# Taps of a convolution spread over three attention heads, its low parts on another engine, and the first queries moved ahead

## The chip, the cores and the metric

The kernel runs on one core of one Trainium2 chip. The metric is the device time of one execution in microseconds (us), as the median of several runs. The engines are TensorE (PE; its weight loads are PEld), VectorE (DVE), ScalarE (ACT), GpSimd (POOL) and SyncE (SP).

## The reference

Two transformer blocks of width 1024 follow each other on 512 latent tokens, with 256 context tokens beside them. The first block has two layers, and the change lies in these. A layer normalises and modulates both token sets, projects them, and mixes them in three ways whose outputs are joined: differential attention with 4 heads, a pooling mixer, and a convolution over 31 taps with a gate before it and a layer norm behind it. The joined mix goes through an output projection, and a feed-forward part follows.

```python
u = a * sigmoid(b)                                  # 256 channels
y = depthwise_conv(u, dw_w, taps=31) + dw_b
conv = silu(layer_norm(y, ln_g, ln_b))
attn = (softmax(q0 k0') - lam * softmax(q1 k1')) v  # 4 heads, queries in blocks of 128
mix  = concat([rms_norm(attn), pool_mixer(u_pool), conv])
x    = x + g1 * (mix @ w_out)
x    = x + g2 * swiglu(modulate(rms_norm(x)))
```

The first layer also carries the context through mix and feed-forward; the second uses it for keys and values alone. The second block (another attention and a recurrence) is not touched.

## The kernel before

Every matrix product keeps 32-bit accuracy by three products: each operand is split into a rounded high part and a low part (the source less the high part), and `mm3` (L250) multiplies high by high, high by low and low by high. `split` (L326) makes the high part on ScalarE and the low part on VectorE, unless another engine is given. Weights are loaded by SyncE in halves, cast by ScalarE (L229) and their low parts taken by GpSimd (L231); `Weights.next` (L234) loads one weight ahead, and there are two buffers for a weight's high and low parts.

Tokens come in three groups of 256: "0" is the context, "1" and "2" the latents. `layer` (L993) of layer 0 begins with `start` (L433), which normalises, and computes the convolution's gate `g` for all tokens and its value `u` for the latents. The context part of `u` is left to the windows. `windows(l)` (L716) gives five lists of items: one before attention, and one for each head. Items are projections of queries and keys (`q0` to `q3`, one a head and token group), of values (`v0`, `v1`), of the pool input (`p`), slices of the modulation (`m`), convolution taps (`t`), the pool mixer (`pool`), the convolution's norm (`ln`), splits of the mix (`sp`) and output parts (`o`). Layer 1 computes the convolution's input at the end of the first list.

`attn` (L873) walks the 4 heads, with 6 query tiles of 128 each in layer 0 and 4 in layer 1. Before every tile it yields, and `layer` emits the next share of the head's list. A tile is `attn_scores` (scores on TensorE into the `s2t` banks, maxima `nmx` on VectorE L800, exponentials `e` on ScalarE L804, the combination of the two softmaxes on VectorE L845) and, one tile later, `attn_values` (transposes, the product with the values, the norm of the output `on` L863 with a square root on GpSimd L298). Queries and keys are normalised by `qk_norm` (L757 on: sums on VectorE L763, square root on GpSimd L298, products on VectorE and GpSimd) and turned on TensorE by `qk_turn` (L792).

The program's text is not the order of the instructions. A planner at build time simulates the engines with durations of its own and takes for each engine, of the instructions that are ready, the one with the best priority; that order is then fixed for every engine. The priority is the place in the text; `high_priority(n)` moves it n places ahead, and a negative n back. Attention is raised by 300.

A tap multiplies the shifted input `uc` by one weight and adds it to `mix[6]` or `mix[7]` (two halves of the channels, `ct` 0 and 1): one VectorE instruction (L665, the first of a half L663) over 783 columns in layer 0 and 512 in layer 1, 62 of them a layer. An item holds 4 taps, and taps are lowered by 1500. The lists of heads 0 and 1 hold 28 and 34 taps. The pool mixer (L612) sums shifted inputs on GpSimd with the `uc` tiles as scratch, and so behind all taps. `splits` (L1026) splits the finished mix for the output projection; output parts with the pool's and the convolution's half of the mix are emitted in head 3.

Of the kernel before, what the change touches and what calls it, by code (L numbers as in the profile page):

```python
# [14 lines left out]
ALU = mybir.AluOpType  # L15
# [11 lines left out]
WINDOWS = (2, 4, 8, 16)  # L27
TAPS = 31
PAD = TAPS // 2
CTX = slice(0, NCX)  # L30
LAT = slice(NCX, NT)

# [210 lines left out]
class K:  # L243
# [365 lines left out]

        return c if self.CW == NX + NCX + PAD and c < NCX else (c + PAD if self.CW != NX else c - NCX)  # L610

    def pool_mix(self, pa, l, ct):  # L612

        nc = self.nc
        add = lambda o, a, b: nc.gpsimd.tensor_tensor(out=o, in0=a, in1=b, op=ALU.add)
        segs, o = [], 0
        for L in ([NCX] if l == 0 else []) + [NX]:
            segs.append((L, self.up[ct][:, o:o + L + 16], self.up[ct][:, o + 8:o + 8 + L]))
            o += L + 16

        def means():
            for L, u, v in segs:
                s = [None] * 4
                prev, ln = u, L + 16
                for i in range(2 if ct == 0 else 4):
                    t = self.uc[i % 2]
                    r = slice(64, 128) if i == 2 * ct + 1 else slice(0, 128)
                    st = 1 << i
                    ln -= st
                    add(t[r, 0:ln], prev[r, 0:ln], prev[r, st:st + ln])  # L630
                    s[i], prev = t, t
                for hf in range(2):
                    i = ct * 2 + hf
                    sh = 8 - WINDOWS[i] // 2
                    r = slice(hf * 64, hf * 64 + 64)
                    tt = self.p_small.tile([128, 2, 8], F32, tag="edge", name="edge", bufs=2)
                    for e in range(2):
                        x0 = e * (L - 8)
                        ed = self.pv("edge", ct * 16 + e * 8, 8)[r]
                        nc.vector.tensor_tensor(out=tt[r, e], in0=s[i][r, sh + x0:sh + x0 + 8], in1=ed, op=ALU.mult)  # L640
                        nc.vector.tensor_tensor(out=tt[r, e], in0=tt[r, e], in1=v[r, x0:x0 + 8], op=ALU.subtract)
                    nc.vector.scalar_tensor_tensor(
                        out=v[r], in0=s[i][r, sh:sh + L], scalar=self.pv("invw", ct)[r], in1=v[r], op0=ALU.mult, op1=ALU.subtract)
                    for e in range(2):
                        nc.vector.tensor_copy(out=v[r, e * (L - 8):e * (L - 8) + 8], in_=tt[r, e])

        def weights():
            for L, _, v in segs:
                ps = self.ps([128, L])
                nc.tensor.matmul(ps, lhsT=self.PW[:, 128 * ct:128 * ct + 128], rhs=v, start=True, stop=True)  # L650
                nc.scalar.activation(out=v, in_=ps, func=AF.Identity, scale=self.pv(f"pscale{l}", ct))

        return [(0, means), (14, weights)]

    def conv_taps(self, pa, l, mix, ct, j0, j1):

        nc = self.nc
        W = self.CW
        m, u = mix[6 + ct][:, 0:W], self.uc[ct]
        dw = lambda j: self.DWH[:, ct * TAPS + j:ct * TAPS + j + 1]  # L660
        for j in range(j0, j1):
            if j == 0:
                nc.vector.tensor_scalar(out=m, in0=u[:, 0:W], scalar1=dw(0), scalar2=self.pv(f"dwb{l}", ct), op0=ALU.mult, op1=ALU.add)  # L663
            else:
                nc.vector.scalar_tensor_tensor(out=m, in0=u[:, j:j + W], scalar=dw(j), in1=m, op0=ALU.mult, op1=ALU.add)  # L665

    def conv_ln(self, pa, l, mix, c, L):

# [47 lines left out]
    def windows(self, l):  # L716

        gr = ("0", "1", "2") if l == 0 else ("1", "2")  # L720
        fm = lambda n: [(n, ct, g) for ct in "01" for g in gr]
        tm = lambda n: [(n, g) for g in "012"]
        taps = [("t", ct, j) for ct in "01" for j in range(0, TAPS, 4)]
        mod = lambda n: [("m",)] * n

        def merge(*ls):

            out = list(ls[0])
            for extra in ls[1:]:
                n, k, r = len(out), 0, []  # L730
                for i, it in enumerate(out):
                    r.append(it)
                    while k < len(extra) * (i + 1) // n:
                        r.append(extra[k])
                        k += 1
                out = r
            return out

        q0, v0 = tm("q0"), tm("v0")
        nm = self.MODS_MIX[l]  # L740
        conv = [it for g in ("01", "2") for n in "gu" for it in fm(n) if it[2] in g]
        return [
            [("u", ct, "0") for ct in "01"] + q0 + v0 if l == 0 else q0[:2] + v0[:2] + q0[2:] + v0[2:] + conv,
            merge(tm("q1") + fm("p"), taps[:7], mod(nm[0])),
            merge(tm("q2") + tm("v1"), taps[7:], mod(nm[1])),
            merge(tm("q3") + [("pool", 0), ("pool", 1)] + [("ln", g) for g in ((0, 1) if l == 0 else (1,))], mod(nm[2])),
            [("sp", int(g), 0) for g in gr] + [("x",)] + mod(nm[3])
            + merge([("o", int(g), m) for g in gr for m in range(KD)], [("sp", int(g), 1) for g in gr]),
        ]
# [76 lines left out]
    def attn_scores(self, pa, l, hd, g, i, qk, og):  # L826

        nc = self.nc
        nk = NCX if g == 0 else NT
        t = slice((2 * g + i) * 128, (2 * g + i) * 128 + 128)  # L830
        s = [self.s2([128, 1024]) for _ in range(2)]
        for n, (a, b) in enumerate(((0, 0), (0, 1), (1, 0))):
            for k0, k1 in ((0, min(nk, 512)), (512, nk)):
                for c in range(2):
                    r = slice(64 * c, 64 * c + 64)
                    if k1 > k0:
                        nc.tensor.matmul(s[c][:, k0:k1], lhsT=qk[r, 0, a, t], rhs=qk[r, 1, b, k0:k1], start=n == 0, stop=n == 2)  # L837
        ss = self.p_small.tile([128, 2], F32, tag="sa", name="sa", bufs=4)
        e = [self.softmax_exp(pa, s[c], nk, ss[:, c:c + 1], f"e{c}") for c in range(2)]

        w = self.p_small.tile([128, 2], F32, tag="rr", name="rr", bufs=4)
        nc.vector.reciprocal(out=w, in_=ss)
        nc.vector.tensor_copy(out=og["r0"][:, i:i + 1], in_=w[:, 0:1])
        nc.vector.scalar_tensor_tensor(out=w[:, 1:2], in0=ss[:, 0:1], scalar=self.LAM[l], in1=w[:, 1:2], op0=ALU.mult, op1=ALU.mult)
        nc.vector.scalar_tensor_tensor(out=e[0][:, 0:nk], in0=e[1][:, 0:nk], scalar=w[:, 1:2], in1=e[0][:, 0:nk], op0=ALU.mult, op1=ALU.add)  # L845
        return e[0], nk

    def attn_values(self, pa, l, hd, g, i, e, nk, v, og, mix):
# [23 lines left out]

    def attn(self, pa, l, qk, v, mix, done):  # L873

        prev = turn = None
        for hd in range(4):
            for g in range(0 if l == 0 else 1, 3):
                for i in range(2):
                    yield hd
                    if i == 0:  # L880
                        og = {n: self.p_small.tile([128, 2], F32, tag="g" + n, name=n, bufs=3) for n in ("r0", "ss")}
                    with self.tc.high_priority(300):
                        e, nk = self.attn_scores(pa, l, hd, g, i, qk[hd], og)
                        if turn is not None:
                            turn()
                        turn = self.attn_values(*prev) if prev is not None else None
                    prev = (pa, l, hd, g, i, e, nk, v[hd], og, mix)
                    if hd == 3 and i == 1 and g > (0 if l == 0 else 1):
                        done(g - 1)
        self.attn_values(*prev)()  # L890
        done(2)
# [101 lines left out]
    def layer(self, l, then):  # L993
# [8 lines left out]
        with self.pool(f"a{l}") as pa, self.pool(f"b{l}") as pb:  # L1002
# [4 lines left out]
            with self.pool(f"mix{l}") as pmix:  # L1007
# [18 lines left out]
                def splits(g, ks):  # L1026
                    for k in ks:
                        src = mix[k] if k not in (4, 5) else self.up[k - 4]
                        o = 8 if k in (4, 5) else 0
                        if g == 0:  # L1030
                            self.split(hmc[k][0], hmc[k][1], src[:, o:o + NCX])
                        else:
                            if full:
                                o += NCX + (16 if k in (4, 5) else 0 if k < 4 else PAD)
                            cs = slice(256 * g - 256, 256 * g)
                            self.split(hm[k][0][:, cs], hm[k][1][:, cs], src[:, o + cs.start:o + cs.stop])

                def issue(it):
                    name = it[0]
# [14 lines left out]
                        return self.mod_slot(*self.mods.pop(0))  # L1054
                    if name == "t":
                        def taps():
                            with self.tc.high_priority(-1500):
                                self.conv_taps(pa, l, mix, int(it[1]), it[2], min(it[2] + 4, TAPS))
                        return taps
                    if name == "pool":  # L1060
                        return self.pool_mix(pa, l, it[1])
                    if name == "ln":
                        return self.conv_ln(pa, l, mix, (0, NCX)[it[1]], (NCX, NX)[it[1]])
                    if name == "x":
# [695 lines left out]
```

## Time and profile before

| | |
|---|---|
| median of 3 runs | 2638.83 us |
| lowest and highest | 2630.06 and 2649.29 us |
| the profiled execution's own time | 2639.62 us |
| its span | 2637.8 us |
| PE busy | 2501.8 us, 95% of the span |
| DVE, ACT, POOL busy | 975.5, 910.5 and 1129.6 us |

Busy times are sums over an engine's instructions; a busy PE is not PE at its peak, so its granted clock (PEclk, as a share of full speed) is read beside it. Rows below are of this one execution, and their times count from the start of its span.

### The profile page before, as it was taken

What the parts mean: (1) busy time and instruction counts of PE and PEld (TensorE: products, weight loads), DVE (VectorE), ACT (ScalarE), POOL (GpSimd) and SP (SyncE); (2) the same over time, 40 slices, a digit from 0 to 9 for tenths busy, and PEclk for the clock granted to TensorE, in tenths of its full rate; (3) what the DMA queues carried; (4) which work ended last, traced back from release to release, by engine and by line L of the source; (5) the groups of instructions that cost most, each with busy time, mean ns of one, the idle gap of its engine ahead of it and who ended that gap; (6) DMA issues with size and microseconds to landing.
All of it is one profiled execution on the core that took longest, in us unless ns stands there. A gap on an engine that the chain in (4) does not pass through costs nothing.

```text
span 2637.8 us, 38665 instructions
## 1 busy us (share of the span) xinstructions
PE 2501.8 (95%) x15840; PEld 2131.7 (81%) x15840; DVE 975.5 (37%) x1941; ACT 910.5 (35%) x1909; POOL 1129.6 (43%) x956
## 2 busy tenths in 40 slices
PE   7889989999999999999989999999998899999998
PEld 5778779988888888877788777778887788888887
DVE  4897564121120224488542112123322756210113
ACT  4334444312112124333535223234444543422222
POOL 4544314433233334555326545445323344555553
PEclk8889989999999999999999999999999899999999
DMA  7113311323223232222224445343101021222221
GB/s 244 58 49 113 122 62 49 113 90 105 93 96 112 85 108 89 75 64 81 97 80 145 152 128 164 116 162 107 52 33 51 17 96 49 80 96 96 93 90 57
DMA packets 68977, 248.55 MB, mean 94 GB/s; under 512 B 7488, under 2 KB 10816, under 8 KB 67136
## 3 DMA queue, kind: packets, MB, share of 16 engines
q1 hardware_dynamic: 65568, 232.29, 27.1%
q10 hardware_dynamic: 3232, 13.79, 1.4%
q8 instruction: 125, 2.05, 0.3%
q14 instruction: 52, 0.43, 0.1%
HBM read 239.75 MB, written 6.29 MB: 93 GB/s over the span
## 4 chain that ended last, share of the span: by engine, by line
PE 48%; DVE 6%; ACT 2%; POOL 1%; DMA 1%; issue 1%; POOLq 0%; ACTq 0%; DVEq 0%; SPq 0%
PE s2t L258 6%; PE s2t L255 6%; PE s2t L259 6%; PE pj L255 5%; PE pj L258 5%; PE pj L259 5%; PE ap L820 2%; DVE mix L665 1%; PE ap L258 1%; PE ap L255 1%; PE ap L259 1%; PE s2t L1532 1%; PE s2t L837 1%; PE ap L344 1%; PE ap L816 1%; PE s L255 1%
## 5 line engine op out<-in xcount | busy, mean ns | idle before, releaser
L231 POOL TENSOR_TENSOR wlo<-raw,whi 128x512 fp32r<-128x512 f32 x564 | 731.2, 1329 | 698.8 <-ACT whi L229 698.5
L229 ACT CAST whi<-raw 128x512 fp32r<-128x512 f32 x576 | 319.7, 616 | 681.9 <-PE pj L258 237.4
L258 PE MATMUL s2t<-hl,whi 128*128 128x512 f32 (+1 forms) x1184 | 448.4, 379 | 0.9 <-POOL hl L429 0.9
L255 PE MATMUL s2t<-hh,whi 128*128 128x512 f32 (+1 forms) x1184 | 447.5, 379 | 0.9 <-ACT whi L229 0.9
L259 PE MATMUL s2t<-hh,wlo 128*128 128x512 f32 (+1 forms) x1184 | 447.0, 378 | 0.0
L255 PE MATMUL pj<-hh,whi 128*128 128x256 f32 (+1 forms) x1088 | 336.6, 311 | 9.9 <-ACT hh L426 3.3
L258 PE MATMUL pj<-hl,whi 128*128 128x256 f32 (+1 forms) x1088 | 331.4, 305 | 2.6 <-DVE hl L431 1.5
L259 PE MATMUL pj<-hh,wlo 128*128 128x256 f32 (+1 forms) x1088 | 330.5, 305 | 0.3 <-POOL wlo L231 0.3
L955 DVE TENSOR_TENSOR sg<-sg,s2t 128x512 f32<-128x512 f32 x66 | 45.4, 688 | 629.2 <-ACT sg L954 629.2
L255 PEld LDWEIGHTS s2t<-hh,whi 128*128 128x128 f32 x1184 | 223.0, 189 | 48.1 <-issue 1.6
L259 PEld LDWEIGHTS s2t<-hh,wlo 128*128 128x128 f32 x1184 | 223.0, 188 | 45.5 <-issue 1.2
L258 PEld LDWEIGHTS s2t<-hl,whi 128*128 128x128 f32 x1184 | 223.0, 188 | 44.8 <-POOL hl L429 1.1
L255 PEld LDWEIGHTS pj<-hh,whi 128*128 128x128 f32 x1088 | 209.3, 193 | 27.5 <-ACT hh L426 4.7
L328 POOL TENSOR_TENSOR gl<-sg,gh 128x512 fp32r<-128x512 f32 (+1 forms) x66 | 97.7, 1480 | 303.9 <-ACT gh L327 303.9
L258 PEld LDWEIGHTS pj<-hl,whi 128*128 128x128 f32 x1088 | 210.1, 193 | 11.5 <-DVE hl L431 1.8
L259 PEld LDWEIGHTS pj<-hh,wlo 128*128 128x128 f32 x1088 | 209.1, 192 | 8.7 <-POOL wlo L231 0.5
L255 PE MATMUL pj<-whi,hh 128*128 128x256 f32 x672 | 198.4, 295 | 1.3 <-ACT v L700 0.9
L259 PE MATMUL pj<-whi,hl 128*128 128x256 f32 x672 | 196.5, 293 | 0.0
L258 PE MATMUL pj<-wlo,hh 128*128 128x256 f32 x672 | 196.5, 292 | 0.0
L894 DVE SCALAR_TENSOR_TENSOR xt<-pj,mod,xt 128x256 f32<-128x256 f32 x224 | 101.7, 480 | 176.2 <-PE pj L259 175.7
L954 ACT ACTIVATE sg<-s2t 128x512 f32<-128x512 f32 x66 | 39.2, 594 | 310.0 <-PE s2t L259 310.0
L258 PE MATMUL pj<-gl,whi 128*128 128x512 f32 (+1 forms) x400 | 145.6, 364 | 0.0
(386 smaller groups left out, 4591.4 us busy)
## 6 DMA issues: line engine op xcount, KB each, us to landing
raw<-in_w_mod SPq DMA_DIRECT2D x144, 512.0 KB, 3.9
raw<-in_w_up SPq DMA_DIRECT2D x132, 512.0 KB, 3.9
raw<-in_w_dn SPq DMA_DIRECT2D x66, 512.0 KB, 4.0
raw<-in_w_in SPq DMA_DIRECT2D x60, 512.0 KB, 3.9
raw<-in_w_out SPq DMA_DIRECT2D x24, 512.0 KB, 3.9
xt<-xs ACTq DMA_DIRECT2D x4, 1024.0 KB, 5.6
xt<-in_xT ACTq DMA_DIRECT2D x2, 1024.0 KB, 7.9
xs<-xt SPq DMA_DIRECT2D x2, 1024.0 KB, 3.9
```

The lines of the kernel that those rows point to most:

```text
L229: nc.scalar.copy(out=h, in_=raw[:, q])
L231: eng.tensor_tensor(out=lo[:, s][:, q], in0=raw[:, q], in1=h.bitcast(F32), op=ALU.subtract)
L255: i = mm(ps, lhsT=lh, rhs=rh, start=start, stop=False)
L258: mm(ps, lhsT=lh, rhs=rl, start=False, stop=False)
L259: return mm(ps, lhsT=ll, rhs=rh, start=False, stop=stop)
L328: (lo_eng or self.nc.vector).tensor_tensor(out=lo, in0=src, in1=hi.bitcast(F32), op=ALU.subtract)
L344: nc.tensor.matmul(ps[g:g + 32], lhsT=self.cond_t[:, k, :], rhs=raw[k // 4][:, k % 4, :], start=k < 4, stop=k >= 4, tile_position=(0, g))
L665: nc.vector.scalar_tensor_tensor(out=m, in0=u[:, j:j + W], scalar=dw(j), in1=m, op0=ALU.mult, op1=ALU.add)
L820: i = nc.tensor.matmul(o, lhsT=at[:, j], rhs=v[:, j0 + j, :], start=j0 + j == 0, stop=j0 + j == nj - 1)
L894: self.nc.vector.scalar_tensor_tensor(out=x, in0=ps, scalar=col, in1=x, op0=ALU.mult, op1=ALU.add)
L954: nc.scalar.activation(out=sg[:, c], in_=p[:, 0], func=AF.Silu)
L955: nc.vector.tensor_tensor(out=sg[:, c], in0=sg[:, c], in1=p[:, 1], op=ALU.mult)
```

## The change

Five edits. (1) `splits` takes the low parts on GpSimd. (2) In layer 0 the first list has the items of `q0` ahead of the context part of `u`. (3) An item holds 2 taps, taps are lowered by 600, and the lists of heads 0, 1 and 2 hold 24, 25 and 13 of them. (4) The first tap of an item is ordered on VectorE behind `self.pace`, the last emitted combination L845; there is none before the first tile. (5) The pool mixer uses `mix[3]` and `uc[0]` as scratch, and the convolution's norm goes behind everything else in the list of head 2.

```diff
-    def pool_mix(self, pa, l, ct):
+    def pool_mix(self, pa, l, ct, scratch):
...
-                    t = self.uc[i % 2]
+                    t = scratch[i % 2]
...
             if j == 0:
-                nc.vector.tensor_scalar(out=m, in0=u[:, 0:W], scalar1=dw(0), ...)
+                i = nc.vector.tensor_scalar(out=m, in0=u[:, 0:W], scalar1=dw(0), ...)
             else:
-                nc.vector.scalar_tensor_tensor(out=m, in0=u[:, j:j + W], ...)
+                i = nc.vector.scalar_tensor_tensor(out=m, in0=u[:, j:j + W], ...)
+            if j == j0 and self.pace is not None:
+                self.order(i, self.pace)
...
-        taps = [("t", ct, j) for ct in "01" for j in range(0, TAPS, 4)]
+        taps = [("t", ct, j) for ct in "01" for j in range(0, TAPS, TAPS_STEP)]      # TAPS_STEP = 2
...
-            [("u", ct, "0") for ct in "01"] + q0 + v0 if l == 0 else ...,
-            merge(tm("q1") + fm("p"), taps[:7], mod(nm[0])),
-            merge(tm("q2") + tm("v1"), taps[7:], mod(nm[1])),
-            merge(tm("q3") + [("pool", 0), ("pool", 1)] + [("ln", g) ...], mod(nm[2])),
+            q0 + [("u", ct, "0") for ct in "01"] + v0 if l == 0 else ...,
+            merge(tm("q1") + fm("p"), taps[:12], mod(nm[0])),
+            merge(tm("q2") + tm("v1"), taps[12:25], mod(nm[1])),
+            merge(tm("q3") + [("pool", 0), ("pool", 1)], taps[25:], mod(nm[2])) + [("ln", g) ...],
...
-        nc.vector.scalar_tensor_tensor(out=e[0][:, 0:nk], in0=e[1][:, 0:nk], ...)
+        self.pace = nc.vector.scalar_tensor_tensor(out=e[0][:, 0:nk], in0=e[1][:, 0:nk], ...)
...
-        prev = turn = None
+        prev = turn = self.pace = None
...
-                            self.split(hmc[k][0], hmc[k][1], src[:, o:o + NCX])
+                            self.split(hmc[k][0], hmc[k][1], src[:, o:o + NCX], nc.gpsimd)
...
-                            self.split(hm[k][0][:, cs], hm[k][1][:, cs], src[:, o + cs.start:o + cs.stop])
+                            self.split(hm[k][0][:, cs], hm[k][1][:, cs], src[:, o + cs.start:o + cs.stop], nc.gpsimd)
...
-                            with self.tc.high_priority(-1500):
-                                self.conv_taps(pa, l, mix, int(it[1]), it[2], min(it[2] + 4, TAPS))
+                            with self.tc.high_priority(-TAPS_LATER):                  # TAPS_LATER = 600
+                                self.conv_taps(pa, l, mix, int(it[1]), it[2], min(it[2] + TAPS_STEP, TAPS))
...
-                        return self.pool_mix(pa, l, it[1])
+                        return self.pool_mix(pa, l, it[1], (mix[3], self.uc[0]))
```

## Rows read from the trace of the kernel before

**Rows 1.** Windows of layer 0: stretch and length, busy us (instructions) by engine, PEclk, DMA
```profile
80.00:100.00 20.00, 20.00 (x170) 20.00 (x170) 19.64 (x20) 4.46 (x8) 11.57 (x7) 1.00 0.33 106
100.00:120.00 20.00, 11.98 (x69) 10.22 (x67) 20.00 (x20) 3.75 (x7) 15.81 (x11) 0.82 0.16 53
120.00:140.00 20.00, 18.63 (x117) 16.53 (x117) 19.48 (x31) 5.08 (x17) 6.00 (x3) 0.84 0.00 1
140.00:160.00 20.00, 20.00 (x120) 17.43 (x120) 17.49 (x23) 8.35 (x21) 7.92 (x5) 0.83 0.18 54
180.00:200.00 20.00, 13.64 (x91) 12.45 (x95) 18.05 (x35) 7.08 (x18) 14.89 (x11) 0.74 0.31 106
220.00:240.00 20.00, 19.93 (x174) 17.18 (x174) 18.34 (x37) 9.67 (x22) 12.37 (x10) 1.00 0.43 142
360.00:380.00 20.00, 14.27 (x92) 13.15 (x93) 12.03 (x35) 10.03 (x30) 0.70 (x1) 0.83 0.40 158
```
**Rows 2.** Windows of layer 1, columns as above (PE, PEld, DVE, ACT, POOL)
```profile
1140.00:1160.00 20.00, 20.00 (x122) 17.45 (x121) 16.69 (x30) 4.88 (x11) 5.48 (x5) 0.83 0.00 1
1160.00:1180.00 20.00, 14.42 (x112) 12.24 (x111) 20.00 (x26) 7.67 (x19) 15.68 (x10) 0.95 0.35 106
1220.00:1240.00 20.00, 13.61 (x92) 12.82 (x91) 18.35 (x36) 6.55 (x16) 14.40 (x12) 0.83 0.09 29
```
**Rows 3.** Tile mix on DVE: durations ns (min/median/max), first and last start; layer 0, layer 1
```profile
L665 DVE SCALAR_TENSOR_TENSOR mix<-uc,DWH,mix x60: 1006/1022/2064, 82.8 to 193.0; 128x783 f32<-128x783 f32 x60
L328 DVE TENSOR_TENSOR hl<-mix,hh x18: 404/416/426, 361.3 to 390.8; 128x256 fp32r<-128x256 f32 x18
L679 DVE SCALAR_TENSOR_TENSOR mix<-pj,mix x4: 414/550/684, 339.0 to 343.1; 128x256 f32<-128x256 f32 x2, 128x512 f32<-128x512 f32 x2
...
L665 DVE SCALAR_TENSOR_TENSOR mix<-uc,DWH,mix x60: 726/740/1849, 1127.1 to 1210.0; 128x512 f32<-128x512 f32 x60
```
**Rows 4.** Timeline of layer 0: start, us, engine, line, tiles [idle before <- releaser]
```profile
88.42 6.88 DVE L665 SCALAR_TENSOR_TENSOR mix<-uc,DWH,mix 128x783 f32<-128x783 f32 x5
89.94 0.61 ACT L761 ACTIVATE sq<-pj 128x512 f32<-128x512 f32 x1
95.23 0.67 DVE L763 TENSOR_REDUCE ss<-sq 128x8 f32<-128x512 f32 x1
...
103.48 0.33 PE L792 MATMUL pj<-ident,y 128*128 128x128 f32 x1 [2.73 <-POOL y L771]
...
120.31 0.74 DVE L800 TENSOR_REDUCE nmx<-s2t 128x1 f32<-128x256 f32 x2
...
121.37 1.46 PE L837 MATMUL s2t<-qk 64*128 64x256 f32 x6 [3.07 <-ACT e L804]
```
**Rows 5.** Windows of DVE by head of layer 0; last row the taps (L665) alone
```profile
80.00:183.00 103.00, 98.51 (x124) 0.89 0.16 50
183.00:252.00 69.00, 57.19 (x135) 0.94 0.33 111
252.00:305.00 53.00, 29.55 (x69) 1.00 0.44 146
305.00:370.00 65.00, 47.00 (x110) 0.91 0.13 44
...
80.00:183.00 103.00, 66.76 (x56) 0.89 0.16 50
```
**Rows 6.** Timeline of ACT and POOL: the first values' weights
```profile
83.74 1.14 ACT L229 CAST whi<-raw 128x512 fp32r<-128x512 f32 x2 [3.98 <-PE pj L259]
84.50 7.15 POOL L231 TENSOR_TENSOR wlo<-raw,whi 128x512 fp32r<-128x512 f32 x4 [2.12 <-ACT whi L229]
```
**Rows 7.** Layer 0: a wait of PE (timeline), and low parts by GpSimd (groups of lines)
```profile
368.35 0.41 PE L868 MATMUL ap<-ident,on 128*128 128x128 f32 x2 [3.20 <-DVE on L863]
...
L429 POOL TENSOR_TENSOR hl<-u,hh 128x256 fp32r<-128x256 f32 x12 | 9.0, 754 | 11.5 <-ACT u L428 11.5
```

More of the change, by code (lines that the diff above doesn't have):

```diff
@@ L29 @@
 PAD = TAPS // 2
+TAPS_STEP = 2
+TAPS_LATER = 600
 CTX = slice(0, NCX)
@@ L662, in conv_taps @@
             if j == 0:
-                nc.vector.tensor_scalar(out=m, in0=u[:, 0:W], scalar1=dw(0), scalar2=self.pv(f"dwb{l}", ct), op0=ALU.mult, op1=ALU.add)
+                i = nc.vector.tensor_scalar(out=m, in0=u[:, 0:W], scalar1=dw(0), scalar2=self.pv(f"dwb{l}", ct), op0=ALU.mult, op1=ALU.add)
             else:
-                nc.vector.scalar_tensor_tensor(out=m, in0=u[:, j:j + W], scalar=dw(j), in1=m, op0=ALU.mult, op1=ALU.add)
+                i = nc.vector.scalar_tensor_tensor(out=m, in0=u[:, j:j + W], scalar=dw(j), in1=m, op0=ALU.mult, op1=ALU.add)
+            if j == j0 and self.pace is not None:
+                self.order(i, self.pace)
     def conv_ln(self, pa, l, mix, c, L):
@@ L742, in windows @@
         return [
-            [("u", ct, "0") for ct in "01"] + q0 + v0 if l == 0 else q0[:2] + v0[:2] + q0[2:] + v0[2:] + conv,
-            merge(tm("q1") + fm("p"), taps[:7], mod(nm[0])),
-            merge(tm("q2") + tm("v1"), taps[7:], mod(nm[1])),
-            merge(tm("q3") + [("pool", 0), ("pool", 1)] + [("ln", g) for g in ((0, 1) if l == 0 else (1,))], mod(nm[2])),
+            q0 + [("u", ct, "0") for ct in "01"] + v0 if l == 0 else q0[:2] + v0[:2] + q0[2:] + v0[2:] + conv,
+            merge(tm("q1") + fm("p"), taps[:12], mod(nm[0])),
+            merge(tm("q2") + tm("v1"), taps[12:25], mod(nm[1])),
+            merge(tm("q3") + [("pool", 0), ("pool", 1)], taps[25:], mod(nm[2])) + [("ln", g) for g in ((0, 1) if l == 0 else (1,))],
             [("sp", int(g), 0) for g in gr] + [("x",)] + mod(nm[3])
@@ L844, in attn_scores @@
         nc.vector.scalar_tensor_tensor(out=w[:, 1:2], in0=ss[:, 0:1], scalar=self.LAM[l], in1=w[:, 1:2], op0=ALU.mult, op1=ALU.mult)
-        nc.vector.scalar_tensor_tensor(out=e[0][:, 0:nk], in0=e[1][:, 0:nk], scalar=w[:, 1:2], in1=e[0][:, 0:nk], op0=ALU.mult, op1=ALU.add)
+        self.pace = nc.vector.scalar_tensor_tensor(out=e[0][:, 0:nk], in0=e[1][:, 0:nk], scalar=w[:, 1:2], in1=e[0][:, 0:nk], op0=ALU.mult, op1=ALU.add)
         return e[0], nk
```

## The prediction

> **What bounds the kernel now.** I read the windows of 20 us first, then the groups of the convolution's tile, then the timeline where TensorE idles, then VectorE by head. The page shows TensorE busy in nearly the whole span, so only time that TensorE loses can be won. For a stretch I count the loss as its length less PE busy times the granted clock. From 80 to 100 us nothing is lost: 170 matmuls in 20 us, 0.118 us each, at clock 1.00. Then in layer 0 the stretches at 100, 120, 140 and 180 us lose 10.2, 4.4, 3.4 and 9.9 us, 27.9 together [rows 1]. In layer 1 those at 1140, 1160 and 1220 us lose 3.4, 6.3 and 8.7, 18.4 together [rows 2]. These are the two stages in which the convolution taps run: all between 82.8 and 193.0 us, and all between 1127.1 and 1210.0 us [rows 3]. [...]
>
> How taps cost TensorE time is seen in the timeline [rows 4]. ScalarE ends the squares of the first query group at 90.55 us; the sum that follows on VectorE starts at 95.23, behind five taps that took 6.88 us. TensorE, which needs the normalised queries to turn them, then waits 2.73 us at 103.48. At 120.31 VectorE gets to the maxima of the first scores, and TensorE has waited 3.07 us for the exponential behind them. VectorE works in the order in which the taps were planned into it, and it runs behind that plan: the median tap takes 1.02 us, the longest 2.06 [rows 3]. From 80 to 183 us it is busy 98.5 of 103 us, 66.8 of them with 56 taps. The next two heads use it 57.2 of 69 and 29.6 of 53 us [rows 5]. That full is no harm by itself: at 220 us VectorE is busy 18.34 of 20 and TensorE loses 0.1 [rows 1].
>
> **The change part by part.** The base is the profiled execution, 2639.6 us (span 2637.8), 0.03% above the median.
>
> Taps. Their work is unchanged, 62 a layer. Before, windows 1 and 2 held 28 and 34, and as fillers all could run when their input was there. Now windows 1, 2 and 3 hold 24, 25 and 13, and each pair (but for two or three pairs in the first slot, when there is no pace yet) stands behind the combination of the tile before. So at most 24 of 62 can be in the first head, 61% leave it. The least that goes is that share, 17.1 us of 27.9 and 11.3 of 18.4. The most is all: with 24 taps at 1.235 us (72.4 us for 60 is the mean; here 66.8/56 = 1.19 is taken, 28.6 us) VectorE's load there falls to 98.5 - 66.8 + 28.6 = 60 of 103 us, far under the fullness that did no harm at 220 us. Between 61 and 100% I take three quarters, since pairs still stand ahead of a late maximum: -20.9 us in layer 0 and -13.8 in layer 1.
>
> The new wait has these behind it on VectorE: nothing but the other taps and, last, the convolution's norm, as the planner may put any ready instruction ahead of a waiting tap. The lower penalty, 600 for 1500, moves taps ahead of what is emitted 600 to 1500 places later; attention, raised by 300, still goes first.
>
> Where the taps go. Head 1 has 57.2 us of VectorE work, 4 or 5 taps (5 us) of it; with 25 at 1.19 it gets 82 for 69 us, so 13 spill over. Head 2 has 29.6 + 15.5 = 45 of 53 us, and takes 8 of them; 5 are left for the fourth head, with 47.0 of 65 [rows 5]. So two heads become as full as the first was. Price, by the nearest rows: at the rate of the first head, 27.9/103 a us, 69 us cost 18.7; at the rate of the stretch at 220 us, 0.1/20, they cost 0.3. I take 6, nearer to the second, because taps now come as pairs behind a tile and not all that are ready at once. Layer 1 has shorter taps, and its price is left in the quarter not won.
>
> First queries ahead. The context part is 48 matmuls, 48 x 0.118 = 5.7 us [rows 1]; the query chain starts up to that much earlier. Against it stands a weight buffer. There are two; the first values' weights take the one that holds the convolution's, and their cast waited for the last context matmul: ScalarE at 83.74, the low parts on GpSimd from 84.50, 7.15 us for four [rows 6]. Now the context part stands behind 144 query matmuls, 17.0 us, so these weights are complete up to 17 us later, near 108 us, when TensorE has only a few turns and the first scores besides. The cost is between -5.7 (lead whole, wait hidden) and +7.9 us (from cast to last low part, 91.65 - 83.74). I take +2: the wait is certain, and the lead is partly in the first term already. On GpSimd those four low parts come while the first query norms want it; on the DMA queue the loads keep their order.
>
> Low parts. 24 subtractions in layer 0 and 16 in layer 1 go from VectorE, median 0.416 us [rows 3], to GpSimd, where the same shape took 0.754 [rows 7]: 10.0 and 6.7 us of VectorE against 18.1 and 12.1 of GpSimd. Between 360 and 380 us GpSimd is busy 0.70 us [rows 1], so it has room. There TensorE waited 3.20 us for the normalised output, with low parts ahead on VectorE [rows 7]; at most this goes. At least nothing: the square root of the same chain is on GpSimd, and queues behind low parts there. I take -3.0, as the planner puts a raised instruction ahead of parts that are merely ready; in layer 1 no such wait stands, 0.
>
> The pool means' new scratch tiles remove a wait for the last taps and add none that ends late: 0. Moving the norm to the end of window 3 is priced with the rival below.
>
> Sum: -20.9 - 13.8 + 6 + 2 - 3 = -29.7; 2639.6 - 29.7 = 2609.9, on the median 2609. Bounds together: -27.9 - 18.4 - 5.7 + 0.3 - 3.2 = -54.9 (2584) and -17.1 - 11.3 + 7.9 + 18.7 + 0 = -1.8 (2637).
>
> [...] Taps took 1.01 us at least and 2.06 at most [rows 3], so something stretches them. [...]
>
> **Rivals.**
> The lag moves along. Heads 1 and 2 at the first head's rate cost 18.7 in place of 6, and layer 1 gives half of its 13.8 back: 2609 + 12.7 + 6.9 = 2629. For it: 82 us of work in 69. Against it: the stretch at 220 us. Chance 0.18.
>
> GpSimd holds up VectorE. If each of the 40 moved low parts stops VectorE for its 0.754 us, that is 30.2 us against the 16.7 taken off: +13.5, and the -3 is gone: 2609 + 16.5 = 2625. [...] Chance 0.06.
>
> The planner undoes it. Order is set by its own durations; if it fills VectorE as before, the time stays at 2639. Chance 0.06.
>
> Slower: the convolution ends too late. Before, the last tap ended at 194 us, and the norm's first step on VectorE came at 339.0, 22.3 us ahead of the first low part of its tile at 361.3 [rows 3]. That slack of 145 us is spent now. Taps of window 3 lose against every attention instruction emitted up to 900 places later, which at 38665 instructions in 2637.8 us is 61 us, a head. If the 13 taps and the 5 us spilled (20 us) all fall into the fourth head, whose VectorE idles 18 of 65 us, the last ends near 370, 31 us after 339; and TensorE has nothing else in that head than output parts, which need this. Layer 1, with 4 tiles a head, gives about half, 15. 2609 + 31 + 15 + 6 = 2661. It decides from a last tap later than 339 us. Against it: head 2 has 8 us of room beyond its own 13 taps. Chance 0.14.
>
> **How the numbers follow.** One per cent, 26.4 us, is about what can be told from no change here. My forecast has 0.56, with 2584 to 2637 as its own range; of it 0.44 lies under 2612.4. Faster is thus 0.44, same 0.12 + 0.18 + 0.06 + 0.06 = 0.42, slower 0.14. The range of 2585 to 2648 leaves out the slower case and little more.
>
> **What would show it.** Right: taps spread over three heads, none but four or six before the first combination; the maxima of the first scores on VectorE within 2 us of the scores; PE above 19 of 20 at clock 1.00 at 100 and 180 us, and at 1160 and 1220. The weight term: the whi cast of the first values near 100 us, and TensorE waiting for wlo soon after. The tail: no wait of TensorE on the normalised output near its low parts, and GpSimd at some 18 us there. Wrong would be waits of some us on maxima in heads 1 and 2, or a convolution norm whose matmul waits for taps.

## The result, and the profile after

The changed kernel takes 2657.78 us (median of 6 runs, 2656.61 to 2659.18) against 2639.77 for the kernel before beside it: ratio 1.007, 95% interval 1.0055 to 1.0084, some 18 us slower. The forecast was 2609 us. The profiled execution after has a span of 2655.5 us, 17.7 more than before.

I read the windows of TensorE by head of layer 0 first; each head ends where the next one's first combination starts, the last with the wait for the output weights' second half. The kernel before, then after; columns are stretch, length, PE busy (instructions), granted clock, DMA share, GB/s.

```profile
60.00:201.00 141.00, 123.44 (x834) 0.89 0.19 60
201.00:264.00 63.00, 61.86 (x525) 1.00 0.35 118
264.00:322.00 58.00, 58.00 (x498) 1.00 0.38 128
322.00:415.00 93.00, 76.07 (x528) 0.91 0.16 57
```

```profile
60.00:193.00 133.00, 122.52 (x819) 0.94 0.19 61
193.00:277.00 84.00, 72.30 (x560) 0.92 0.30 100
277.00:332.00 55.00, 53.30 (x455) 1.00 0.36 118
332.00:433.00 101.00, 77.68 (x549) 0.88 0.15 54
```

The first head is 8 us shorter, the second 21 longer, the third 3 shorter, the fourth with the tail 8 longer: 355 us became 373. That is all of the 17.7 us; behind layer 0 the gains and losses of this profile cancel.

The windows of 20 us, after (they answer to [rows 1]; columns as there):

```profile
100.00:120.00 20.00, 17.70 (x121) 16.32 (x121) 18.24 (x27) 6.55 (x19) 11.53 (x8) 0.88 0.25 82
120.00:140.00 20.00, 20.00 (x102) 15.46 (x101) 6.10 (x7) 2.84 (x8) 0.00 (x0) 0.83 0.00 1
180.00:200.00 20.00, 19.38 (x152) 17.31 (x152) 19.43 (x34) 8.83 (x26) 13.03 (x10) 0.91 0.33 109
220.00:240.00 20.00, 11.51 (x100) 10.08 (x99) 19.71 (x38) 5.58 (x13) 13.71 (x9) 0.87 0.31 106
```

At 100 and 180 us TensorE is better fed than in [rows 1]; at 220, where nothing was lost before, it loses 10.0 us (20 - 11.51 x 0.87). The groups of the tile mix on VectorE, after (they answer to [rows 3]), and VectorE in the first two heads (to [rows 5], with the bounds moved along with the heads):

```profile
L670 DVE SCALAR_TENSOR_TENSOR mix<-uc,DWH,mix x60: 1015/1030/2048, 102.5 to 309.8; 128x783 f32<-128x783 f32 x60
L644 DVE TENSOR_TENSOR edge<-mix,PV x8: 149/150/1216, 190.0 to 224.5; 64x8 f32<-64x8 f32 x8
L686 DVE SCALAR_TENSOR_TENSOR mix<-pj,mix x4: 415/552/691, 352.9 to 357.7; 128x256 f32<-128x256 f32 x2, 128x512 f32<-128x512 f32 x2
```

```profile
80.00:177.00 97.00, 61.55 (x92) 0.93 0.13 41
177.00:264.00 87.00, 77.84 (x158) 0.90 0.30 99
```

So the taps did move: the last one starts at 309.8, not 193.0, and the first head's VectorE is busy 61.55 us in place of 98.51. What else is in the second head is shown by the pool mixer's step on `mix` (L644): it runs from 190.0 to 224.5, while the taps run. The timeline of VectorE, and one row of TensorE, in that stretch:

```profile
234.16 1.02 DVE L670 SCALAR_TENSOR_TENSOR mix<-uc,DWH,mix 128x783 f32<-128x783 f32 x1
235.22 0.75 DVE L646 SCALAR_TENSOR_TENSOR up<-uc,PV,up 64x512 f32<-64x512 f32 x1
...
236.08 1.82 DVE L807 TENSOR_REDUCE nmx<-s2t 128x1 f32<-128x768 f32 x2
```

```profile
238.97 2.28 PE L844 MATMUL s2t<-qk 64*128 64x512 f32 x6 [8.01 <-ACT e L811]
```

TensorE waits 8.01 us for an exponential, whose maxima VectorE reaches at 236.08, behind taps and pool steps in turn.

### The profile page after: what moved, and what is told of

It is laid out like the page before. It is cut to its first block, busy times and chain, and to the rows that moved or that the text cites. A ratio compares the mean times of both kernels' runs of the same rounds, so it can differ in the third digit from the quotient of the medians.

```text
span 2655.5 us, 38647 instructions
## 1 busy us (share of the span) xinstructions
PE 2506.5 (94%) x15840; PEld 2133.8 (80%) x15840; DVE 962.2 (36%) x1901; ACT 908.5 (34%) x1909; POOL 1159.2 (44%) x996
## 3 DMA queue, kind: packets, MB, share of 16 engines
q1 hardware_dynamic: 65568, 232.29, 26.9%
## 4 chain that ended last, share of the span: by engine, by line
PE 48%; DVE 5%; ACT 2%; POOL 1%; issue 1%; DMA 1%; POOLq 0%; ACTq 0%; DVEq 0%; SPq 0%
PE s2t L261 6%; PE s2t L258 6%; PE s2t L262 6%; PE pj L258 6%; PE pj L261 5%; PE pj L262 5%; PE ap L827 2%; PE ap L261 1%; PE ap L258 1%; PE ap L262 1%; PE s2t L1539 1%; PE s2t L844 1%; PE ap L347 1%; DVE mix L670 1%; PE s L258 1%
## 5 line engine op out<-in xcount | busy, mean ns | idle before, releaser
L262 PE MATMUL pj<-gh,wlo 128*128 128x512 f32 (+1 forms) x400 | 145.4, 364 | 0.0
```

The costliest lines, as they stand in the source:

```text
L262: return mm(ps, lhsT=ll, rhs=rh, start=False, stop=stop)
```

## The experiments

Besides its ratio each kernel is given at equal clock: all runs list span and mean granted clock, and about each kernel's own mean a clock lower by 0.001 goes with 1.57 us more span (a fit over all runs). So spans are carried to 0.974, the mean of before's 76 runs in these comparisons, and before's own (2636.4) is taken off. The changed kernel is +19.3 at equal clock. What an edit does through the clock itself is left out of such a figure, so it does not replace the ratio. Lengths of single heads and layers are those of one profile each, and differ by some us where nothing was changed: layer 1, from TensorE's first wait of some 2 us for queries to turn to its wait for the output weights, takes 281.0 us before, and, with the same text, 282.7 in a2 and 276.8 in d4.

**a1**, edit 1 alone:

```diff
-self.split(hmc[k][0], hmc[k][1], src[:, o:o + NCX])
+self.split(hmc[k][0], hmc[k][1], src[:, o:o + NCX], nc.gpsimd)   # and the latents'
```

> The kernel before with the low parts of the mix on GpSimd and nothing else changed. Theory A (memory): the loads of the residual go into memory of the early pool, which is free only when the last low part of the pool's and the convolution's half is done; on GpSimd that is later (80.5 ns more than 300 a piece, 0.754 against 0.416 us, in one queue), so the load lands later and TensorE waits for the first flushes: 9.9 us in layer 0 and 3.5 in layer 1 of the changed kernel, so 8 to 13 us slower than before. Rival B (the tail is not at fault, the taps are): within 3 us of before. My prediction had 3 us faster.

(The figure in the parenthesis is a slip: a part takes 0.416 us on VectorE and 0.754 on GpSimd.) Measured: 1.0051 [1.0034, 1.0068], but +2.7 us at equal clock: its four runs were granted 0.968 to 0.970, before's 0.970 to 0.978. Whether the planner's new order or chance made that clock low stays open.

**a2**, edit 2 alone (`q0` ahead of the context part):

> The kernel before with the first queries ahead of the context part and nothing else changed. In the changed kernel the first scores came at 96.1 us in place of 106.1. Theory: with all taps free to run from the start the queries' norm is still behind taps, so 2 to 6 us faster at most. Rival (the weight buffer held longer costs what the lead gives): within 2 us, or up to 8 us slower.

Measured: 1.0027 [1.0013, 1.0041], +3.3 at equal clock.

**a3**, the taps and the pool mixer's scratch (edits 3 to 5), without 1 and 2:

> The changed kernel with low parts on VectorE and the old first order: the taps' edits and the new scratch alone. Theory C (collision): head 1 now has taps and the pool mixer's steps at once, and VectorE is over 18.5 of 20 us busy from 200 to 240 us; what the first head wins (about 11 us from 80 to 200 us, some of it from the first queries) is less than what heads 1 and 2 lose (17 us from 200 to 320 us): 3 to 12 us slower than before. Rival B (taps are sound and the low parts alone lose): 5 to 15 us faster than before.

Measured: 1.003 [1.0016, 1.0043], +8.0 at equal clock. Already this part, meant as the gain, is a loss, and its second head has a wait of 7.99 us.

**a4**, the changed kernel without edit 1:

> The changed kernel with the low parts back on VectorE. Theory A: the wait of 9.9 us on the first flush in layer 0 and of 3.5 us in layer 1 go, 8 to 13 us faster than the changed kernel, 5 to 10 us slower than before. Rival (the wait is for a late convolution, not for low parts): within 3 us of the changed kernel.

Measured: 1.0074 [1.0059, 1.0089]; +14.1 at equal clock. By ratio the low parts cost nothing here.

**b1**, only the first query group ahead of the context part:

```diff
-q0 + [("u", ct, "0") for ct in "01"] + v0
+q0[:1] + [("u", ct, "0") for ct in "01"] + q0[1:] + v0
```

> The changed kernel, with the context part of the convolution behind the first of the three query groups in place of behind all three. Theory D (the two edits clash through a weight buffer): with the taps spread, TensorE has no other work when the first values' weights come late, because their buffer is the convolution's and is free only behind the context part; so here the first head ends earlier, and most of the 11 us between the taps alone and taps with the new lead come back: 6 to 11 us faster than the changed kernel. Rival (the clash is in the planner's order elsewhere): within 3 us of the changed kernel.

Measured: 1.0049 [1.0034, 1.0064], +13.5: a part of the way back.

**b2**, the changed kernel with the pool mixer behind the last tap, on its old scratch:

```diff
-merge(tm("q3") + [("pool", 0), ("pool", 1)], taps[25:], mod(nm[2])) + [("ln", ...
+merge(tm("q3"), taps[25:], mod(nm[2])) + [("pool", 0), ("pool", 1)] + [("ln", ...
-self.pool_mix(pa, l, it[1], (mix[3], self.uc[0]))
+self.pool_mix(pa, l, it[1], self.uc)
```

> The changed kernel, with the pool mixer behind the last tap and on its old scratch tiles, as the order was before. Theory C (taps and mixer collide in head 1): TensorE's wait of 8.0 us at 239 us goes, and the 17 us lost in head 1 fall to under 6; some comes back as a later mixer in head 3: 5 to 12 us faster than the changed kernel. Rival (25 taps are too many for head 1 with or without the mixer): head 1 still loses over 10 us, within 3 us of the changed kernel.

Measured: 1.0013 [1.0002, 1.0025], +7.4, so 12 of the 19 us are back. In the trace the first of the mixer's eight passes still runs at 192.6 to 200.8, and the others from 282.95 to 315, behind the last tap. TensorE by head of layer 0 in b2:

```profile
60.00:188.00 128.00, 117.51 (x779) 0.95 0.18 60
188.00:260.00 72.00, 68.81 (x566) 0.95 0.35 114
260.00:329.00 69.00, 63.38 (x495) 0.98 0.29 97
329.00:425.00 96.00, 76.17 (x516) 0.88 0.16 56
```

The wait of 8 us in the second head is gone and the head is 12 us shorter, but the third is 14 longer: the two take 141 us, against 139 in the changed kernel. So the 12 us don't lie there. By these profiles 5 lie in the first head, 5 in the last with the tail, and the rest behind layer 0.

**b3**, the changed kernel without the order of pairs behind tiles (the call of `self.order` taken out):

> The changed kernel without the order of tap pairs behind the tiles' combinations: the pairs are fillers as before, lowered by 600. If the order is what spreads the taps, they run earlier again and the first head loses more (over 25 us in place of 18), head 1 less: 0 to 6 us faster than the changed kernel. If the item lists do it, nothing moves: within 3 us.

Measured: 1.006 [1.0045, 1.0075], +16.6. The loss goes back into the first head: from 60 us on 26.9 us are lost there and 2.5 in the second, against 18.3 and 17.3 in the changed kernel (length less busy time by clock, in windows of 10 us). Layer 0 ends 7 us earlier than in the changed kernel (its last wait, for the output weights' second half, is over at 425.84 against 432.89), and layer 1 is 8 us longer (287.1 against 278.7). The order decides where the time is lost, and changes the total by 0.001.

**b4**, the changed kernel without edit 2:

> The changed kernel with the old first order: the taps' edits and the low parts on GpSimd. Theory D: the new lead costs 8 to 12 us in this company though it cost less by itself, so 8 to 12 us faster than the changed kernel, 6 to 10 us slower than before. With theory A (low parts) true as well, TensorE's wait on the first flush, 9.9 us, would still be there; if the low parts cost as little here as between the changed kernel and the one without them, the time is that of the taps alone plus 0 to 3 us.

Measured: 1.0035 [1.0021, 1.0048], +11.6.

**c1**, the taps spread and paced, with the mixer and the norm at the end of head 2's list, and nothing else: a3 with b2's edit:

> The changed kernel with only its taps spread and paced: low parts back on VectorE, the first order back as before, and the pool means put back behind the last tap on their old scratch tiles. Theory one, the pool means between taps spoil head 1 and everything else of the spreading is a gain: the taps with the early pool means alone gave 1.003; 8 to 13 us less of loss in head 1 (16.9 to 5.9 where the pool means were moved behind in the whole change) brings that to 0.998 to 1.000, and with a shorter first head no more than before's own loss elsewhere, so 0.996 to 1.000. Theory two, two more full heads cost by themselves what the first head gains, whatever the pool means do: 1.003 again. Theory three, the pool means behind the last tap end too late for the last head: over 1.005, with TensorE waiting for them after head 3.

Measured: 1.0017 [1.0004, 1.003], +2.5. Theory one's size fell: with the pool mixer behind the taps the spread still wins nothing.

**c2**, the kernel before with the new scratch alone:

```diff
-return self.pool_mix(pa, l, it[1])
+return self.pool_mix(pa, l, it[1], (mix[3], self.uc[0]))
```

> The kernel before, with the pool means on the new scratch tiles alone. There all taps end by 193 us and the first pool step could come at 188 in the changed kernel, 194 in the kernel before. Theory one, only pool steps that stand between taps cost: 1.000, within 0.001. Theory two, the new scratch has a price of its own (the fourth kind's values or the outputs wait for the tile): 1.002 or more, and a wait of some us on that tile.

Measured: 1.0041 [1.0026, 1.0057], +5.1 (half of it with a lower clock, 0.9705). The profile shows no wait on that tile, so theory two's reason is not shown either. In it layer 0 ends 3.5 us earlier than before (412.12 against 415.60), and layer 1 is 11 us longer (292.2 against 281.0), at a granted clock of 0.92 in place of 0.95: by this profile the price of the scratch lies where no tap was moved, and its cause is not settled.

**c3**, b2 without edit 2:

> The changed kernel with the pool means behind the last tap on their old scratch (1.0013) and the first order back as before; low parts stay on GpSimd. Theory one, the first queries ahead cost by themselves 7 us (alone 1.0027) wherever the rest stands: 0.9985, and the low parts on GpSimd cost 0 to 5 us against the run without them. Theory two, the first order matters only with the pool means in the way: 1.0013 again.

Measured: 1.0021 [1.001, 1.0032], +2.9. Against it b2, which has edit 2, is 0.0008 faster by ratio and 4.5 us slower at equal clock, so the times leave it open. The two traces tell more than either. VectorE and TensorE in b2, then in c3:

```profile
94.68 0.39 PE L844 MATMUL s2t<-qk 64*128 64x256 f32 x2 [2.35 <-ACT qk L330]
100.08 0.42 DVE L595 SCALAR_TENSOR_TENSOR uc<-sb,pj 128x256 f32<-128x256 f32 x1 [3.36 <-PE pj L262]
100.54 0.69 DVE L668 TENSOR_SCALAR mix<-uc,DWH,PV 128x783 f32<-128x783 f32 x1
101.27 2.10 DVE L670 SCALAR_TENSOR_TENSOR mix<-uc,DWH,mix 128x783 f32<-128x783 f32 x2
...
105.28 0.74 DVE L807 TENSOR_REDUCE nmx<-s2t 128x1 f32<-128x256 f32 x2
111.39 1.45 DVE L852 SCALAR_TENSOR_TENSOR e<-e,rr 128x256 f32<-128x256 f32 x1
```

```profile
102.11 0.38 PE L844 MATMUL s2t<-qk 64*128 64x256 f32 x2 [2.36 <-ACT qk L330]
103.68 0.75 DVE L807 TENSOR_REDUCE nmx<-s2t 128x1 f32<-128x256 f32 x2
106.37 0.48 DVE L852 SCALAR_TENSOR_TENSOR e<-e,rr 128x256 f32<-128x256 f32 x1
```

The first scores come 7.4 us earlier with edit 2, and the first combination 5.0 us later. VectorE's order has the context part of `uc` ahead of the first maxima; that part is now behind the queries, so VectorE idles 3.36 us for it, then works off three taps that it set free, and reaches the maxima 10.6 us after the scores in place of 1.6. The taps are not what delays it: with all but the first tap of each half left out (d2 against d1, below) the scores come at 97.08 in place of 102.61, and the first combination at 111.82 in place of 106.86. Nor does the delay last in this pair: the second head's first combination comes at 188.22 in b2 and at 188.15 in c3.

**c4**, c1 with 24, 15 and 23 taps in place of 24, 25 and 13:

> As the run with the taps alone and the pool means behind them, but five pairs (10 taps) of the second window go to the third: 24, 15 and 23 of 62. Theory one, VectorE's room by head is what counts (head 1 has 11.8 us left, head 2 23.4, the fourth 18): 5 us less loss in head 1, 1 to 2 more later, 3 us better than that run. Theory two, the late convolution norm sets the end: 5 us or more worse, the last tap after 339 us.

Measured: 1.0013 [1.0004, 1.0023], +6.1. No better than c1, and 3.6 us slower at equal clock. In the profiles heads 1 and 2 take 64 and 85 us, in c1 71 and 72: the loss goes where the taps go.

**d1 and d2**, the kernel before and the changed kernel with 60 of 62 taps a layer left out:

```diff
-for j in range(j0, j1):
+for j in range(j0, min(j1, 1)):
```

> The kernel before with 60 of the 62 taps of each layer left out (only the first tap of each half is computed, so the convolution's output is wrong): what all of them cost TensorE together, the ceiling of any spreading. Theory one, by the prediction: 46.3 us are lost in the front stretches of the two layers because of taps, so 35 to 46 us are gained, 0.982 to 0.987. Theory two, the front stretches of the attention stay short of other work and TensorE waits there for the exponential and the maxima with or without taps, so that spreading had little to win: 15 us or less, 0.994 to 0.999, with a loss of over 15 us still standing between 60 us and the second head.

> The changed kernel with the same 60 of 62 taps left out of each layer: the price of the other edits when no tap is in their way. Theory one, pool steps, low parts and first queries cost only where they meet taps on VectorE: within 0.001 of the kernel before without taps. Theory two, they cost by themselves what they cost alone (7.5 us for the low parts less 7 us that lie in an untouched stretch, 7 for the first queries, up to 5 for the scratch): 0.003 to 0.006 above the kernel before without taps.

Measured: d1 0.9912 [0.9896, 0.9929], -18.9; d2 0.9941 [0.9929, 0.9953], -13.0. Both of d1's theories fell: all taps together cost 23 us (19 to 27), neither 35 to 46 nor under 15. This is what the program gains without them; the planner orders the rest anew. And without these taps the other edits still cost 0.0029, 6 to 8 us; in the profiles the first head of layer 0 is where d2 is longer, 127 us against 113. TensorE by head of layer 0 in d1, and last all heads of its layer 1:

```profile
60.00:173.00 113.00, 108.55 (x789) 0.97 0.20 64
173.00:238.00 65.00, 65.00 (x545) 1.00 0.39 128
238.00:298.00 60.00, 60.00 (x516) 1.00 0.36 124
298.00:393.00 95.00, 77.59 (x532) 0.89 0.16 56
...
1069.00:1339.00 270.00, 254.33 (x1847) 0.95 0.24 82
```

333 us in place of 355: 22 us are saved here, the first head being 28 shorter and the others 2 each longer, and the last head with its tail loses 26 us (95 - 77.59 x 0.89) with hardly a tap left. Layer 1 takes 270 us, against 275 before.

**d3 and d4**, c1's spread in layer 1 alone and in layer 0 alone; the other layer as before (windows of 28 and 34, fours, no order, lowered by 1500):

> The kernel before with the taps of layer 1 alone spread over three heads and paced, and the pool means behind them; layer 0 as before. Theory one, spreading wins where a head has four tiles and shorter taps (in the profile of the spread in both layers, layer 1 was 8 us shorter and layer 0 unchanged): 0.996 to 0.998. Theory two, the loss moves to later heads in both layers: 1.000 to 1.001.

> The same for layer 0 alone, layer 1 as before. Theory one, the loss moves from the first head to the second, third and fourth in full: 0.999 to 1.002. Theory two, spreading wins here too and layer 1 or a stretch behind it spoils it where both are spread: 0.995 to 0.998.

Measured: d3 0.9968 [0.9956, 0.998], -6.8, **faster than both kernels**, 2630.79 us; d4 1.0028 [1.0018, 1.0038], +7.3. Their edits together are c1's. Their times add up to -1.0 us by ratio and +0.5 at equal clock, where c1 has +4.5 and +2.5; by ratio the gap is about as wide as the intervals. Layer 0 by head in d4; then the first three heads of layer 1, the kernel before and d3:

```profile
60.00:187.00 127.00, 120.35 (x788) 0.91 0.18 61
187.00:259.00 72.00, 68.65 (x555) 0.93 0.34 112
259.00:331.00 72.00, 66.15 (x510) 0.95 0.29 95
331.00:423.00 92.00, 74.29 (x508) 0.89 0.16 58
```

```profile
1090.00:1198.00 108.00, 100.18 (x737) 0.95 0.22 69
1198.00:1253.00 55.00, 48.55 (x352) 0.94 0.24 77
1253.00:1316.00 63.00, 59.43 (x448) 0.97 0.30 99
```

```profile
1087.00:1181.00 94.00, 88.39 (x675) 0.96 0.21 68
1181.00:1239.00 58.00, 55.63 (x423) 0.97 0.27 92
1239.00:1307.00 68.00, 59.58 (x446) 0.92 0.28 93
```

In layer 0 the first head gives 14 us and heads 1 and 2 take 9 and 14. In layer 1 the first gives 14 too, and heads 1 and 2 take only 3 and 5; with the fourth, layer 1 goes from 275 to 267 us. That is 3 us less than with hardly a tap (d1), which is not explained and no more than profiles differ by.

## Why the prediction was wrong

**The taps' term failed, by 33 of the 49 us.** It was -20.9 - 13.8 + 6 = -28.7; c1, which is that term alone, gave 1.0017, about +4.5 (+2.5 at equal clock). Two steps of it fell.

"The least that goes is that share" took the whole 46.3 us lost in the front stretches for the taps' doing, because TensorE idled there behind taps. d1 shows that all taps cost 23 us; the rest is lost without them. By the profiles that is 22 us of layer 0, where the step claimed 27.9, and some 5 of layer 1, where it claimed 18.4. A wait whose last releaser is a tap is not gone with the tap: what is late next was never asked for the front, though the prediction asked it for the tail.

"I take 6" for two fuller heads is the larger miss. It leaned on one stretch, 220 to 240 us, in which VectorE was 18.34 of 20 busy without harm [rows 1]. The 18.7 beside it is the first head's rate over 69 us, one head's length; over both, 69 and 53 us, that rate gives 33. In d4 heads 1 and 2 are 23 us longer and by the prediction's own count lose 17.4 us (8.2 and 9.2; before 1.1 and 0); the rest goes mostly with 42 more matmuls that stand in them. TensorE waits there for turned queries (2.90 us) and for a normalised output (3.79), and the granted clock is 0.93 and 0.95. The first head gave 14 us, not 20.9. So layer 0 alone came to +7.4 in place of -14.9, two thirds of the taps' miss, and layer 1 to -8.4 (-6.8 at equal clock) in place of -13.8.

The rival "the lag moves along" had -20.9 + 18.7 = -2.2 for layer 0 and half of 13.8, -6.9, for layer 1. It was right about layer 1, and in layer 0 right about the mechanism; there it too forecast a gain, as it kept the 20.9.

**"The pool means' new scratch tiles remove a wait for the last taps and add none that ends late: 0."** The 0 was wrong. The wait removed was what kept the pool mixer out of the taps. b2 puts it back: 1.007 to 1.0013, 12 us at equal clock and 15 by ratio; from a3 to c1 it is 5.5 and 3.4, and the new scratch alone (c2) costs 5.1 and 10.8. In the changed kernel the mixer's 188 to 239 us fall into the head with most taps, alternate between GpSimd and VectorE, and stand ahead of the maxima for which TensorE waits 8.01 us. That this collision is the price is not shown: in b2 the third head loses what the second wins, and c2 loses its time in layer 1. Which wait the mixer's place costs stays open. What the traces do show is that removing a wait on one engine let in work on another: the step that moves was priced, the steps that become ready with it weren't.

**First queries ahead, +2.** Alone +0.0027; in the other three pairs +0.0044 (a3 to a4), +0.0035 (b4 to the changed kernel) and -0.0008 (c3 to b2), at equal clock 3.3 to 7.7 in all four. The sign was right and the cause wrong: the first values' weights are cast at 93.37 in place of 83.74 [rows 6], right behind the last query matmul and not behind the context part; their low parts are complete at 100.65, TensorE uses them from 105.92, and no wait of over 1 us for them is in the trace. What the traces show instead is VectorE's order at the first maxima, above for b2 and c3. How much of the cost it is stays open: when the second head begins, 5 us of delay are left in the changed kernel against b4 (192.67 and 187.50), and none in b2 against c3. In the changed kernel the first scores come at 96.08 and their maxima at 106.67, so "within 2 us of the scores" was wrong by 8.6 us. Why the whole change pays most for it isn't settled.

**Low parts, -3.** The 3.20 us of [rows 7] were to go, "as the planner puts a raised instruction ahead of parts that are merely ready". That step failed. With the low parts alone moved (a1) the same wait is 3.44 us; GpSimd's low parts and square root there, then TensorE:

```profile
362.29 5.35 POOL L328 TENSOR_TENSOR hl<-mix,hh 128x256 fp32r<-128x256 f32 x6
367.59 0.70 POOL L298 TENSOR_TENSOR ray<-rav,mhalf 128x2 f32<-128x2 f32 x1
...
369.61 0.66 PE L868 MATMUL ap<-ident,on 128*128 128x128 f32 x2 [3.44 <-DVE on L863]
```

The square root's input is there at 365.60, and it starts behind six low parts. In the changed kernel it has its input at 381.96 and starts behind nine, and another wait of TensorE stands before its result is used. TensorE, VectorE, the DMA issue of the residual on ScalarE's queue, and GpSimd, after:

```profile
388.08 0.58 PE L258 MATMUL pj<-hh,whi 128*128 128x256 f32 x1 [9.90 <-DVE xc L901]
...
387.54 0.88 DVE L901 SCALAR_TENSOR_TENSOR xc<-pj,mod,xc 128x256 f32<-128x256 f32 x2 [5.58 <-DMA xc<-in_cT]
...
L1566 ACTq DMA_DIRECT2D xc<-in_cT x1: 335/335/335, 382.6 to 382.6; - x1
...
381.90 5.90 POOL L331 TENSOR_TENSOR hl<-mix,hh 128x256 fp32r<-128x256 f32 x9
387.76 0.69 POOL L301 TENSOR_TENSOR ray<-rav,mhalf 128x2 f32<-128x2 f32 x1
```

The residual `xc` takes memory that the early pool (`up`, `mix`) gives back, so by these times its load waits for the last low part of `up`, which now ends on GpSimd at 381.93; before, the load went out at 366.95. TensorE then waits 9.90 us; the normalised output is there only at 389.10, so the late load alone is not shown to cost that. In a4 that wait is gone and one of 5.78 us on the normalised output stands there. By ratio the edit is worth nothing either way in company (-0.0004, +0.0005, +0.0004 from a4, a3 and c1), and 13.5 us alone (a1); at equal clock it costs 5.2, 3.6 and 0.4 us in company and 2.7 alone. No pair shows a gain at equal clock. The 18.2 us of GpSimd (17 low parts in 11.5 us and 6 in 6.7, from 360 to 400 us) were as forecast (18.1). The rival "GpSimd holds up VectorE" put 13.5 us more on these parts; a1 has that by ratio, but most of it goes with a lower clock, and no other pair has it.

**The slower case** had the right sign, and with 2661 nearly the time, by luck: its mechanism did not come. It asked for a last tap later than 339 us, and the last one starts at 309.8. The convolution's norm came 13.9 us late (352.9), of which 10.6 are the later start of its head (332.26 against 321.67).

**Other marks.** "The planner undoes it" fell: taps lie from 102.5 to 309.8. Four taps stand before the first combination, as forecast. TensorE above 19 of 20 at clock 1.00 came at neither 100 nor 180 us, nor at 1160 and 1220 (16.34 at 0.92 and 17.13 at 1.00). A mark of being wrong did come: the wait of 8.01 us behind maxima in head 1.

## What to carry to other kernels

Before pricing work as the cause of idle time, run the kernel without that work: here it was worth 23 us, not 46. The price of moving filler work into a later stretch is that stretch's loss when full, measured for each layer on its own; the same spread won 8.4 us in one and lost 7.4 in the other. When a dependency is removed, ask what else becomes ready with it, on which queue, and what it will stand ahead of there.

## What the runs showed of the hardware

Two small steps of VectorE took 1.18 and 1.22 us beside a GpSimd instruction, and ended within 0.03 us of its end. Two rows of VectorE, with the same step at 0.20 and 1.18 us, and GpSimd's beside the second:

```profile
214.11 0.20 DVE L851 SCALAR_TENSOR_TENSOR rr<-sa,lam,rr 128x1 f32<-128x1 f32 x1
...
228.63 1.18 DVE L851 SCALAR_TENSOR_TENSOR rr<-sa,lam,rr 128x1 f32<-128x1 f32 x1
...
226.82 2.98 POOL L234 TENSOR_TENSOR wlo<-raw,whi 128x512 fp32r<-128x512 f32 x2
```

The long one ends at 229.81, and GpSimd's second subtraction at 229.80; the median of the 40 steps of that line is 0.21 us, which the step at 358.64 us took too, beside GpSimd's square root (358.54 to 359.25). Pool steps of 64x8 took 0.15 to 1.22 us (the group of L644 above), and the longest ends likewise, at 191.27 beside a GpSimd instruction that ends at 191.24. What holds the step, the traces do not show. Whether the mixer's steps are dearer among taps for it, and how much of b2's 12 us that would be, was not measured.

The granted clock was 0.83 at 120 to 140 us after, with PE busy 20.00 of 20, behind the stretch at 100 in which it was busy 17.70 of 20 at 0.88. Of the 46.3 us that the prediction counted as lost in the kernel before, 27.7 are idle time of PE (20 less PE busy, over its stretches in [rows 1] and [rows 2]) and the other 18.6 a granted clock of 0.74 to 0.95.
